# 138 extra 128x128 products of constants on TensorE in the two mixing stages of a diffusion trunk

## The chip, the cores and the metric

The program runs on one core of one Trainium2 chip. A core has TensorE (PE in the profile; its weight loads are PEld), VectorE (DVE), ScalarE (ACT), GpSimd (POOL) and SyncE (SP, which issues most transfers). The metric is the device time of one execution in microseconds, lower is better. The kernel before took 1597.66 us, the median of three runs (1592.06 to 1597.91).

## The reference, cut to what matters

Two layers; in each a half-step SwiGLU, the token mixing, and another half-step SwiGLU, for 128 context tokens and 256 latent tokens (384 columns in all). Only the mixing is touched:

```python
def token_mix(h, lp, lam_init, ctx, pos):
    a_q, a_k, a_v, b_q, b_k, b_v, b_g, b_r, c_q, c_k, c_v = jnp.split(h @ lp['w_in'], offs, axis=-1)
    # a: 6 query heads of 64 over 2 key heads; c: 4 heads, each with two score maps of 48
    # latent tokens: rope_2d on a_q, a_k, c_q, c_k; their keys are the latent and the cached context keys
    out_a = gqa_attention(a_q, keys_a, vals_a)            # softmax(q k / 8) v
    o_b, s_f, s_b = gla_bidir(b_q, b_k, b_v, log_a_f, log_a_b, s0_f, s0_b)   # gated linear attention, chunks of 64
    out_b = rms_norm(o_b, lp['g_gla']) * jax.nn.silu(b_r)
    # c: w = softmax(q1 k1) - lam * softmax(q2 k2);  out_c = rms_norm(w v)
    out_c = rms_norm(diff_attention(c_q, keys_c, vals_c, lam), lp['g_c_out']) * (1.0 - lam_init)
    return jnp.concatenate([out_a, out_b, out_c], axis=-1) @ lp['w_out']
```

## The kernel before

Activations lie transposed, 128 features by 384 tokens. Every big product is made of three passes (`mm3`, lines 307 to 310): the fp32 weights are split into a high and a low part (ScalarE line 303, VectorE line 304), and high by high, high by low and low by high are added in PSUM. So the four SwiGLU stages (FFN) and the projections of the mixing are long rows of dense 128-row passes, while the attention itself is plain fp32, in which one call of `PE.matmul` is two passes in the trace (an xcount of 2).

The mixing (`mixing`, lines 561 to 1085) is cut into named stages, and `ORDER[l]` lists them by layer: projections (`wq`, `wk`, `bv`, `wa`, `wv` in `proj_m`), norms and rotary embedding with a transpose behind it (`a_rope`, `c_rope`, lines 1002 and 1035), the levels of the gated attention (`L0` to `L6`, `scores`, line 901: 32-row products), the four heads of the differential attention (`c0` to `c3`, `c_head`), the pairs of grouped heads (`p0` to `p2`, `a_probs`), and the output product over `wo`. The code is written in that order, and a scheduler that simulates the engines lays the instructions out: an instruction of a later stage may be put ahead where its operands and buffers are there, and on each engine the laid-out order is then fixed.

A head of `c_head` does, for each of two blocks of 128 queries: two score products on 64 rows (line 789), on each a maximum (VectorE, line 694), an exponential with its sum (ScalarE, line 697), a reciprocal, scaling (lines 794 and 797) and three transposes (line 721, copied out by ScalarE, line 722); then the products with the values (lines 801 and 803, 128 rows) and a sum of squares by a product with ones (line 807). PSUM has eight banks: three of the tag `mm` and `both` by turns for big products and scores, three of `ax` and `ada` for the rest; a bank is taken anew when its last reader is done.

`ones` and `ident` are 128x128 constants in SBUF.

Of the kernel before, what the change touches and what calls it, by code (L numbers as in the profile page):

```python
# [17 lines left out]
P = 128  # L18
# [4 lines left out]
T = SEQ + LAT  # L23
# [58 lines left out]
def _build(ctx, tc, nc, I, O):  # L82
# [224 lines left out]
    def mm3(ps, lh, ll, rh, rl, start, stop):  # L307
        PE.matmul(ps, lhsT=lh, rhs=rh, start=start, stop=False)  # L308
        PE.matmul(ps, lhsT=lh, rhs=rl, start=False, stop=False)  # L309
        return PE.matmul(ps, lhsT=ll, rhs=rh, start=False, stop=stop)  # L310

    def newton(pool, ss, n, scale, parts, tag):

        m = pool.tile([P, n], F32, tag=tag + "m", name="nm")[:parts]
        V.tensor_scalar(out=m, in0=ss, scalar1=scale, scalar2=EPS, op0=ALU.mult, op1=ALU.add)
        s = pool.tile([P, n], I32, tag=tag + "s", name="ns")[:parts]
        V.tensor_scalar(out=s, in0=m.bitcast(I32), scalar1=1, scalar2=None, op0=ALU.logical_shift_right)
        y = pool.tile([P, n], F32, tag=tag + "y", bufs=2, name="ny")[:parts]
        V.tensor_scalar(out=y.bitcast(I32), in0=s, scalar1=-1.0, scalar2=float(0x5f3759df), op0=ALU.mult, op1=ALU.add)
        mh = pool.tile([P, n], F32, tag=tag + "h", name="nh")[:parts]  # L320
        V.tensor_scalar(out=mh, in0=m, scalar1=-0.5, scalar2=None, op0=ALU.mult)
        for _ in range(3):
            a = pool.tile([P, n], F32, tag=tag + "a", name="na")[:parts]
            V.tensor_tensor(out=a, in0=y, in1=y, op=ALU.mult)
            V.tensor_tensor(out=a, in0=a, in1=mh, op=ALU.mult)
            y2 = pool.tile([P, n], F32, tag=tag + "y", bufs=2, name="ny")[:parts]
            V.scalar_tensor_tensor(out=y2, in0=a, scalar=1.5, in1=y, op0=ALU.add, op1=ALU.mult)
            y = y2
        return y
# [231 lines left out]
    def mixing(l, us, acc, nxt):  # L561
        turn["own"] = {"mm": ("both",), "ax": ("ada",)}
        r_ = make_rstd(acc)
        with tc.tile_pool(name=f"mix{l}", bufs=1) as mp:
# [3 lines left out]
            def t512(n=512):  # L568
                return mt([P, 512], "t5", N512)[:, :n]


            kta = mt([P, T], "kta")
            ktc = mt([P, 4, 512], "ktc")
# [33 lines left out]
                    S.activation(out=dst[:, a:b], in_=t[:, a:b], func=func, bias=bc[:, c:c + 1], scale=scale)  # L607

            def proj_m(name, n, kper):
                ps = [mmps()[:, :n] for _ in range(3)]  # L610
                for k0 in range(0, KT, kper):
                    w = load_split(I[name][l, k0 // kper], kper * n)
                    for k in range(k0, k0 + kper):
# [123 lines left out]
            def a_probs(i):  # L737

                pts = [mt([P, 3, LAT], "pt", NPT), mt([P, 3, LAT], *(("e", 3) if i else ("pt", NPT)))]
                for t in range(2):  # L740
                    pp = [mmps()[:, :T] for _ in range(2)]
                    for g in range(2):
                        r = slice(64 * g, 64 * g + 64)
                        PE.matmul(pp[g], lhsT=qta[r, i, (t + 1) * P:(t + 2) * P], rhs=kta[r, :], start=True, stop=True)
                    for g, (p, rs) in enumerate(map(smax, pp)):
                        S.activation(out=p, in_=p, func=AF.Copy, scale=rs)
                        to_pt(p.rearrange("p (a b) -> p a b", a=3), 3, pts[g][:, :, t * P:(t + 1) * P])
                return pts
# [34 lines left out]
            def c_head(h, oc, osq, pss):  # L783
                pt = mt([P, 3, LAT], "pt", NPT)
                for t in range(2):
                    pp = [(mmps if PMM[4] else axps)()[:, :T] for _ in range(2)]
                    for m in range(2):
                        r = slice(64 * m, 64 * m + 64)
                        PE.matmul(pp[m], lhsT=qtc[r, h, (t + 1) * P:(t + 2) * P], rhs=ktc[r, h, 0:T],  # L789
                                  start=True, stop=True)  # L790
                    (p0, r0), (p1, r1) = map(smax, pp)
                    V.tensor_tensor(out=r1, in0=r1, in1=nl, op=ALU.mult)
                    if NRM[1]:
# [99 lines left out]
            sc = [mt([P, 2, 3, P], f"sc{i}") for i in range(2)]  # L893

            def scores(q, k, h, cross):
                ps = (mmps if PMM[10] else axps)()[:, :192].rearrange("p (c t) -> p c t", c=3)
                r = slice(32 * h, 32 * h + 32)
                for c in range(3):
                    for f in range(2):
                        fq = 1 - f if cross else f  # L900
                        PE.matmul(ps[64 * f:64 * f + 64, c, :], lhsT=k[r, c * P + 64 * f:c * P + 64 * f + 64],  # L901
                                  rhs=q[r, c * P + 64 * fq:c * P + 64 * fq + 64], start=True, stop=True)
                return ps

            def gla_diag():
# [75 lines left out]
                    V.tensor_tensor(out=lo, in0=ot[:, i, :], in1=hi.bitcast(F32), op=ALU.subtract)  # L981
                    mob.append((P, hi, lo))

            sv = {}

            def a_proj():
                pa = proj_m("wa", 512, 2)
                sv["a"] = qk_norm(pa, ((0, 6, 64, gq[:, 0:64]), (384, 2, 64, gq[:, 64:128])), 8, 64)
# [1 line left out]
            def a_rope():  # L990
                xa, ra = sv["a"]
                for t in range(3):
# [4 lines left out]
                    else:  # L997
                        xr = xa[0].rearrange("p h d -> p (h d)")
                        nc.sync.dma_start(out=O["nak"][l], in_=xr[:, 384:512])
                    ps = (mmps if PMM[13] else axps)()  # L1000
                    for i in range(4):
                        PE.transpose(ps[:, i * P:(i + 1) * P], xr[:, i * P:(i + 1) * P], ident)
                    S.activation(out=qta[:, :, t * P:(t + 1) * P],
# [17 lines left out]
            def c_rope(w):  # L1021
                xc, rc = sv[w]
                for t in range(3):
# [6 lines left out]
                    else:  # L1030
                        V.tensor_tensor(out=xc[t], in0=xc[t], in1=rc[t], op=ALU.mult)
                        rope(pad[:, :, 0:48], xc[t], 8, 48, t - 1, K_CC, K_SC)
                    ps = (mmps if PMM[13] else axps)()
                    for h in range(4):
                        PE.transpose(ps[:, h * P:(h + 1) * P], pad[:, 2 * h:2 * h + 2, :].rearrange("p a b -> p (a b)"),
                                     ident)
# [34 lines left out]
            acc = new_acc()  # L1071
            us = []
            for m in range(KT):
                ps = mmps()[:, :T]
                for k0, k1 in ((0, 5), (5, 9)):
                    w = load_split(I["wo"][l, m][:, k0 * P:k1 * P], (k1 - k0) * P)
                    for k in range(k0, k1):
# [141 lines left out]
```

## Time and profile before

| | |
|---|---|
| profiled execution | 1599.75 us |
| its span (first to last instruction) | 1597.9 us |
| TensorE busy | 1563.3 us (98%) |
| VectorE, ScalarE, GpSimd busy | 1229.3 (77%), 738.8 (46%), 196.2 (12%) us |
| mean granted TensorE clock | 0.980 of full |
| chain that ended last | TensorE 90%, VectorE 6%, ScalarE 2% |

The page gives busy time, the span in 40 slices with the granted clock, the chain of waits and the costliest groups. TensorE's ends are modelled, so a busy TensorE need not stream at its peak. The clock has two levels, 2.4 GHz (1.00 in the profile) and 1.2 GHz (0.50). Slices 10 to 13 (to about 520 us) and 28 to 33 (from about 1110 to 1290 us) hold the two mixings.

### The profile page before, as it was taken

What the parts mean: (1) busy time and instruction counts of PE and PEld (TensorE: products, weight loads), DVE (VectorE), ACT (ScalarE), POOL (GpSimd) and SP (SyncE); (2) the same over time, 40 slices, a digit from 0 to 9 for tenths busy, and PEclk for the clock granted to TensorE, in tenths of its full rate; (3) what the DMA queues carried; (4) which work ended last, traced back from release to release, by engine and by line L of the source; (5) the groups of instructions that cost most, each with busy time, mean ns of one, the idle gap of its engine ahead of it and who ended that gap; (6) DMA issues with size and microseconds to landing.
All of it is one profiled execution on the core that took longest, in us unless ns stands there. A gap on an engine that the chain in (4) does not pass through costs nothing.

```text
span 1597.9 us, 25055 instructions
## 1 busy us (share of the span) xinstructions
PE 1563.3 (98%) x9370; PEld 1464.0 (92%) x9370; DVE 1229.3 (77%) x2294; ACT 738.8 (46%) x1444; POOL 196.2 (12%) x239
## 2 busy tenths in 40 slices
PE   7999999999999999999999999999999999999999
PEld 5999999997558999999999999999875699999999
DVE  4799999888766888898968889667787767666532
ACT  4544433365466544443344444335546754444321
POOL 1211130030000211111001111102000011111100
PEclk9999999999789999999999999999898999999999
DMA  9677778542104566666666666543321064443441
GB/s 330 231 229 229 226 225 261 165 122 83 45 1 140 168 197 202 201 192 207 204 213 197 210 197 195 174 144 96 113 77 39 1 230 144 143 137 130 120 143 57
DMA packets 83230, 256.38 MB, mean 160 GB/s; under 512 B 10978, under 2 KB 19746, under 8 KB 82722
## 3 DMA queue, kind: packets, MB, share of 16 engines
q1 hardware_dynamic: 83108, 254.78, 50.3%
q8 instruction: 74, 1.21, 0.3%
q14 instruction: 48, 0.39, 0.1%
HBM read 251.99 MB, written 2.75 MB: 159 GB/s over the span
## 4 chain that ended last, share of the span: by engine, by line
PE 90%; DVE 6%; ACT 2%; issue 1%; DMA 1%; POOL 1%; SPq 0%; DVEq 0%; ACTq 0%; POOLq 0%
PE mm L308 20%; PE mm L310 20%; PE mm L309 20%; PE both L308 7%; PE both L309 7%; PE both L310 7%; PE mm L789 1%; DVE wlo L304 1%; PE ax L803 1%; PE ax L901 1%; PE ax L721 1%; DVE junk L254 1%; PE ax L807 0%; DVE ht L397 0%; PE ax L758 0%
## 5 line engine op out<-in xcount | busy, mean ns | idle before, releaser
L303 ACT ACTIVATE whi<-wraw 128x1024 fp32r<-128x1024 f32 (+4 forms) x358 | 348.4, 975 | 461.2 <-PE mm L309 259.1
L304 DVE TENSOR_TENSOR wlo<-wraw,whi 128x1024 fp32r<-128x1024 f32 (+4 forms) x358 | 451.8, 1264 | 131.0 <-ACT whi L303 129.0
L310 PE MATMUL mm<-h,wlo 128*128 128x386 f32 x1096 | 373.3, 341 | 2.5 <-DVE wlo L304 2.5
L308 PE MATMUL mm<-h,whi 128*128 128x386 f32 x1096 | 372.8, 341 | 2.6 <-POOL h L367 1.4
L309 PE MATMUL mm<-h,whi 128*128 128x386 f32 x1096 | 372.5, 340 | 0.0
L254 DVE SCALAR_TENSOR_TENSOR junk<-araw,cb 128x1024 f32<-128x1024 f32 x256 | 312.3, 1220 | 0.8
L310 PEld LDWEIGHTS mm<-h,wlo 128*128 128x128 f32 x1096 | 208.0, 190 | 4.2 <-DVE wlo L304 3.5
L308 PEld LDWEIGHTS mm<-h,whi 128*128 128x128 f32 x1096 | 207.6, 190 | 4.6 <-ACT whi L303 1.7
L309 PEld LDWEIGHTS mm<-h,whi 128*128 128x128 f32 x1096 | 207.6, 189 | 1.6 <-issue 0.7
L477 POOL TENSOR_TENSOR alo<-s,ahi 128x384 fp32r<-128x384 f32 x88 | 115.5, 1314 | 641.5 <-ACT ahi L475 614.9
L309 PE MATMUL mm<-alo,whi 128*128 128x384 f32 x528 | 177.9, 337 | 0.0
L310 PE MATMUL mm<-ahi,wlo 128*128 128x384 f32 x528 | 177.9, 337 | 0.0
L308 PE MATMUL mm<-ahi,whi 128*128 128x384 f32 x528 | 177.9, 337 | 0.0
L308 PE MATMUL both<-h,whi 128*128 128x386 f32 x360 | 122.5, 340 | 0.0
L309 PE MATMUL both<-h,whi 128*128 128x386 f32 x360 | 122.1, 339 | 0.0
L310 PE MATMUL both<-h,wlo 128*128 128x386 f32 x360 | 122.0, 339 | 0.0
L475 ACT ACTIVATE ahi<-s 128x384 fp32r<-128x384 f32 x88 | 46.3, 526 | 129.4 <-DVE s L472 129.3
L309 PEld LDWEIGHTS mm<-alo,whi 128*128 128x128 f32 x528 | 99.2, 188 | 0.0
L310 PEld LDWEIGHTS mm<-ahi,wlo 128*128 128x128 f32 x528 | 99.2, 188 | 0.0
L308 PEld LDWEIGHTS mm<-ahi,whi 128*128 128x128 f32 x528 | 99.2, 188 | 0.0
L469 DVE TENSOR_TENSOR u<-mm,rstd 128x384 f32<-128x384 f32 x66 | 36.6, 554 | 60.8 <-PE mm L310 60.8
L467 ACT ACTIVATE s<-s,bc 128x128 f32<-128x128 f32 (+1 forms) x176 | 70.7, 449 | 8.0 <-ACT bc L418 0.7
(365 smaller groups left out, 2446.7 us busy)
## 6 DMA issues: line engine op xcount, KB each, us to landing
wraw<-in_wgu SPq DMA_DIRECT2D x170, 512.0 KB, 4.2
araw<-in_w_adat SPq DMA_DIRECT2D x128, 512.0 KB, 4.0
wraw<-in_wd SPq DMA_DIRECT2D x64, 512.0 KB, 4.2
wraw<-in_wd SPq DMA_DIRECT2D x32, 384.0 KB, 3.5
araw<-in_w SPq DMA_DIRECT2D x16, 512.0 KB, 5.6
wraw<-in_wo SPq DMA_DIRECT2D x16, 320.0 KB, 3.0
wraw<-in_wit SPq DMA_DIRECT2D x8, 512.0 KB, 3.4
wraw<-in_wa SPq DMA_DIRECT2D x8, 512.0 KB, 3.6
```

Of the source, the lines that this page charges most:

```text
L254: V.scalar_tensor_tensor(out=junk, in0=w, scalar=1.0, in1=self.cb[:, c, :], op0=ALU.mult, op1=ALU.mult, accum_out=self.acc[:, f, c:c + 1])
L303: S.activation(out=hi[:, :cols], in_=raw[:, :cols], func=AF.Copy)
L304: vi = V.tensor_tensor(out=lo[:, :cols], in0=raw[:, :cols], in1=hi[:, :cols].bitcast(F32), op=ALU.subtract)
L308: PE.matmul(ps, lhsT=lh, rhs=rh, start=start, stop=False)
L309: PE.matmul(ps, lhsT=lh, rhs=rl, start=False, stop=False)
L310: return PE.matmul(ps, lhsT=ll, rhs=rh, start=False, stop=stop)
L467: S.activation(out=s[:, a:b], in_=s[:, a:b], func=AF.Silu, bias=bg[:, c:c + 1])
L469: vi = V.tensor_tensor(out=u, in0=pu[:, :T], in1=r, op=ALU.mult)
L475: S.activation(out=hi, in_=s, func=AF.Copy)
L477: G.tensor_tensor(out=lo, in0=s, in1=hi.bitcast(F32), op=ALU.subtract)
L721: pi = PE.transpose(ps[:, i * P:(i + 1) * P], p[:, i, :], ident)
L789: PE.matmul(pp[m], lhsT=qtc[r, h, (t + 1) * P:(t + 2) * P], rhs=ktc[r, h, 0:T], start=True, stop=True)
```

## The change

A helper `warm(ps, n, c)` issues n products of `ones` with `ident` into 128 columns of a PSUM tile that nobody reads, from column c on (384 by default, behind the 384 columns that scores use). Sixty-nine are issued in each mixing: 4 into the first bank of the first `proj_m`; 1 after each two of four heads' scores in the gated attention, so 2 in each of its eight rounds; 8 before the first scores of head `c0`; 1 on each score tile of the heads (16) and of the grouped heads (12); 1 before each rotary transpose (9); 4 before the first output product. The score tiles are therefore taken whole and cut to 384 columns afterwards; else nothing is changed.

```diff
+    def warm(ps, n, c=384):
+        for _ in range(n):
+            PE.matmul(ps[:, c:c + P], lhsT=ones, rhs=ident, start=True, stop=True)
...
             def proj_m(name, n, kper):
-                ps = [mmps()[:, :n] for _ in range(3)]
+                ps = [mmps() for _ in range(3)]
+                if not sv.setdefault("pm", 0):
+                    warm(ps[0], 4, 0)
+                sv["pm"] += 1
+                ps = [p[:, :n] for p in ps]
...
             def a_probs(i):
...
+                    for p in pp:
+                        warm(p, 1)
...
             def c_head(h, oc, osq, pss):
                 pt = mt([P, 3, LAT], "pt", NPT)
                 for t in range(2):
-                    pp = [(mmps if PMM[4] else axps)()[:, :T] for _ in range(2)]
+                    pp = [(mmps if PMM[4] else axps)() for _ in range(2)]
+                    if h == t == 0:
+                        warm(pp[0], 8)
                     for m in range(2):
...
+                    for p in pp:
+                        warm(p, 1)
+                    pp = [p[:, :T] for p in pp]
                     (p0, r0), (p1, r1) = map(smax, pp)
...
             def scores(q, k, h, cross):
-                ps = (mmps if PMM[10] else axps)()[:, :192].rearrange("p (c t) -> p c t", c=3)
+                bk = (mmps if PMM[10] else axps)()
+                ps = bk[:, :192].rearrange("p (c t) -> p c t", c=3)
...
+                if h % 2:
+                    warm(bk, 1)
...
                     ps = (mmps if PMM[13] else axps)()
+                    warm(ps, 1)          # in a_rope and in c_rope, before the transposes
...
             for m in range(KT):
-                ps = mmps()[:, :T]
+                ps = mmps()
+                if m == 0:
+                    warm(ps, 4)
+                ps = ps[:, :T]
```

The lines of the changed file are 5 to 25 higher; the products are its line 315. Three places of TensorE's order follow.

Where head `c0` begins in layer 0, before: the last level rounds (line 901), the scores of `c0` (line 789) and the first transposes (line 721).

```order
L901 MATMUL ax<-e 64x64 x6
L901 MATMUL ada<-e 64x64 x6
L901 MATMUL ax<-e 64x64 x12
L789 MATMUL mm<-ktc,qtc 128x384 x2
L789 MATMUL both<-ktc,qtc 128x384
L789 MATMUL mm<-ktc,qtc 128x384 x3
L789 MATMUL both<-ktc,qtc 128x384
L789 MATMUL mm<-ktc,qtc 128x384
L721 MATMUL ax<-cst,p 128x128 x3
```

The same place now (901 is 921, 789 is 805, 721 is 732).

```order
L921 MATMUL ax<-e 64x64 x12
L315 MATMUL ax<-cst 128x128
L315 MATMUL mm<-cst 128x128 x8
L805 MATMUL mm<-ktc,qtc 128x384 x2
L315 MATMUL mm<-cst 128x128 x2
L805 MATMUL both<-ktc,qtc 128x384
L805 MATMUL mm<-ktc,qtc 128x384
L315 MATMUL both<-cst 128x128
L315 MATMUL mm<-cst 128x128
L805 MATMUL mm<-ktc,qtc 128x384 x2
L315 MATMUL mm<-cst 128x128 x2
```

Eight products stand before the first scores, and a pair behind each pair of scores, ahead of the first transposes.

A little later, before: `c0`'s transposes, three scores of head `c1` put ahead, and `c0`'s products with the values (801, 803).

```order
L801 MATMUL ax<-ptx,cv 96x128
L789 MATMUL mm<-ktc,qtc 128x384 x2
L721 MATMUL ada<-cst,p 128x128 x3
L789 MATMUL both<-ktc,qtc 128x384
L803 MATMUL ax<-pt,cv 96x256 x3
L901 MATMUL ada<-e 64x64 x6
L789 MATMUL mm<-ktc,qtc 128x384
L807 MATMUL ax<-pt,cst 96x384
L901 MATMUL ax<-e 64x64 x12
```

The same place now (801 is 820, 803 is 822, 807 is 826).

```order
L805 MATMUL mm<-ktc,qtc 128x384
L315 MATMUL mm<-cst 128x128
L805 MATMUL both<-ktc,qtc 128x384
L822 MATMUL ax<-pt,cv 96x256 x3
L921 MATMUL ada<-e 64x64 x6
L315 MATMUL ada<-cst 128x128
L805 MATMUL mm<-ktc,qtc 128x384
L826 MATMUL ax<-pt,cst 96x384
L921 MATMUL ax<-e 64x64 x18
L315 MATMUL ax<-cst 128x128
L732 MATMUL ax<-cst,p 128x128 x3
```

The third score tile of `c1` (`both`) is still ahead, but the product in its bank is not: it stands further down, behind all that is shown here.

At the rotary transposes of `wk` in layer 0, before (1035 are the transposes, 309 and 310 passes of the projection `wa`).

```order
L901 MATMUL ax<-e 64x64 x18
L901 MATMUL ada<-e 64x64 x6
L1035 MATMUL ax<-cst,t_4125 128x128 x4
L309 MATMUL mm<-wlo,h 128x512
L310 MATMUL mm<-whi,h 128x512
L1035 MATMUL ax<-cst,t_4135 128x128 x4
```

The same place now (1035 is 1057).

```order
L921 MATMUL ada<-e 64x64 x6
L315 MATMUL ada<-cst 128x128
L315 MATMUL ax<-cst 128x128
L1057 MATMUL ax<-cst,t_4136 128x128 x4
L315 MATMUL ax<-cst 128x128
L1057 MATMUL ax<-cst,t_4147 128x128 x4
L315 MATMUL ax<-cst 128x128
```

A product stands right before each group of four transposes, and the passes that stood between two groups now stand behind both.

## Rows read from the trace of the kernel before

**Rows 1.** Page, parts 0 and 2: span, and granted clock in 40 slices

```profile
span 1597.9 us, 25055 instructions
...
PEclk9999999999789999999999999999898999999999
```

**Rows 2.** Windows at the low clock: start:end, length, busy us (instructions), clock, DMA

```profile
387.40:390.80 3.40, 3.40 (x16) 2.89 (x15) 3.05 (x7) 1.84 (x11) 0.00 (x0) 0.50 0.44 150
421.50:448.80 27.30, 26.83 (x112) 13.60 (x110) 15.07 (x46) 14.27 (x37) 0.00 (x0) 0.50 0.00 1
479.50:482.90 3.40, 3.40 (x11) 2.35 (x10) 2.81 (x6) 3.22 (x10) 0.00 (x0) 0.50 0.02 5
1118.00:1121.20 3.20, 3.20 (x15) 3.20 (x15) 2.71 (x5) 0.29 (x1) 0.00 (x0) 0.50 0.60 156
1128.10:1134.80 6.70, 6.70 (x30) 6.14 (x31) 4.59 (x14) 3.90 (x11) 0.00 (x0) 0.50 0.02 7
1179.30:1182.60 3.30, 3.30 (x12) 2.19 (x12) 2.12 (x6) 0.60 (x1) 0.00 (x0) 0.50 0.32 84
1213.40:1227.00 13.60, 13.60 (x42) 6.66 (x42) 7.26 (x23) 8.01 (x21) 0.00 (x0) 0.50 0.00 0
1271.50:1274.80 3.30, 3.30 (x13) 3.30 (x13) 1.44 (x4) 2.71 (x8) 0.00 (x0) 0.50 0.00 0
sum 64.20, PE 63.73 PEld 40.32 DVE 39.04 ACT 34.83 POOL 0.00; mean PE 7.97 PEld 5.04 DVE 4.88 ACT 4.35 POOL 0.00
```

**Rows 3.** Windows: a projection, two before a fall, one cold, warm heads

```profile
392.00:414.00 22.00, 22.00 (x98) 17.80 (x98) 20.01 (x45) 8.91 (x12) 2.37 (x2) 1.00 0.21 58
418.10:421.40 3.30, 0.84 (x5) 0.49 (x4) 3.25 (x11) 1.48 (x5) 0.00 (x0) 1.00 0.45 141
430.00:448.00 18.00, 18.00 (x92) 9.68 (x91) 8.66 (x26) 8.15 (x21) 0.00 (x0) 0.50 0.00 0
...
1124.70:1128.00 3.30, 3.30 (x45) 2.07 (x44) 1.54 (x3) 3.27 (x7) 0.00 (x0) 1.00 0.56 187
1228.00:1264.00 36.00, 35.03 (x320) 21.41 (x318) 28.18 (x100) 28.57 (x80) 2.01 (x4) 1.00 0.01 2
```

**Rows 4.** Timeline of TensorE before the fall at 1128: start, us, engine, line, shapes

```profile
1125.32 0.91 PE L634 MATMUL ax<-p 32*128 32x384 f32 x2
...
1126.80 1.26 PE L901 MATMUL ax<-qk 32*64 32x64 f32 x36
```

**Rows 5.** Timeline of TensorE, line 803 alone: one row each head

```profile
431.18 2.87 PE L803 MATMUL ax<-pt,cv 128*96 128x256 f32 x6
...
444.37 2.87 PE L803 MATMUL ax<-pt,cv 128*96 128x256 f32 x6
...
452.35 1.53 PE L803 MATMUL ax<-pt,cv 128*96 128x256 f32 x6
...
1231.42 1.54 PE L803 MATMUL ax<-pt,cv 128*96 128x256 f32 x6
...
1237.80 1.53 PE L803 MATMUL ax<-pt,cv 128*96 128x256 f32 x6 [0.47 <-ACT pt L722]
```

**Rows 6.** Chain of waits in order of time: one 128-column product, cold and warm

```profile
425.56 0.43 PE ax L801 x2
...
1230.44 0.22 PE ax L801 x2
```

**Rows 7.** Timeline of TensorE: its waits, in brackets, with what ended them

```profile
381.00 0.63 PE L1035 MATMUL ax<-cst,t 128*128 128x128 f32 x4 [0.82 <-DVE t L688]
...
420.65 1.96 PE L789 MATMUL mm<-ktc,qtc 64*128 64x384 f32 x4 [2.46 <-ACT p L697]
...
477.46 0.91 PE L744 MATMUL both<-kta,qta 64*128 64x384 f32 x2 [1.62 <-ACT e L965]
...
1117.05 0.40 PE L309 MATMUL mm<-wlo,h 128*128 128x288 f32 x1 [1.88 <-DVE wlo L304]
...
1211.38 2.03 PE L789 MATMUL mm<-ktc,qtc 64*128 64x384 f32 x6 [1.15 <-ACT p L697]
```

More of the change, by code (lines that the diff above doesn't have):

```diff
@@ L569, in t512 @@
                 return mt([P, 512], "t5", N512)[:, :n]
+            sv = {}
             kta = mt([P, T], "kta")
@@ L740, in a_probs @@
                 for t in range(2):
-                    pp = [mmps()[:, :T] for _ in range(2)]
+                    pp = [mmps() for _ in range(2)]
                     for g in range(2):
                         r = slice(64 * g, 64 * g + 64)
-                        PE.matmul(pp[g], lhsT=qta[r, i, (t + 1) * P:(t + 2) * P], rhs=kta[r, :], start=True, stop=True)
-                    for g, (p, rs) in enumerate(map(smax, pp)):
+                        PE.matmul(pp[g][:, :T], lhsT=qta[r, i, (t + 1) * P:(t + 2) * P], rhs=kta[r, :], start=True,
+                                  stop=True)
+                    for p in pp:
+                        warm(p, 1)
+                    for g, (p, rs) in enumerate(smax(p[:, :T]) for p in pp):
                         S.activation(out=p, in_=p, func=AF.Copy, scale=rs)
@@ L785, in c_head @@
                 for t in range(2):
-                    pp = [(mmps if PMM[4] else axps)()[:, :T] for _ in range(2)]
+                    pp = [(mmps if PMM[4] else axps)() for _ in range(2)]
+                    if h == t == 0:
+                        warm(pp[0], 8)
                     for m in range(2):
                         r = slice(64 * m, 64 * m + 64)
-                        PE.matmul(pp[m], lhsT=qtc[r, h, (t + 1) * P:(t + 2) * P], rhs=ktc[r, h, 0:T],
+                        PE.matmul(pp[m][:, :T], lhsT=qtc[r, h, (t + 1) * P:(t + 2) * P], rhs=ktc[r, h, 0:T],
                                   start=True, stop=True)
+                    for p in pp:
+                        warm(p, 1)
+                    pp = [p[:, :T] for p in pp]
                     (p0, r0), (p1, r1) = map(smax, pp)
@@ L982, in gla_out @@
                     mob.append((P, hi, lo))
-            sv = {}
             def a_proj():
@@ L1033, in c_rope @@
                     ps = (mmps if PMM[13] else axps)()
+                    warm(ps, 1)
                     for h in range(4):
```

## The prediction, made before the changed kernel was run

> **What bounds the kernel now.** I read the page first. TensorE is busy for nearly all of the span of 1597.9 us, and its granted clock is full but for a few slices, all in the two mixings [rows 1]. So the question is what those slices cost, and the windows view, cut until a window held one level only, answers it: TensorE ran at 1.2 GHz in eight stretches, 64.2 us together, and in them it was busy for 63.7 us [rows 2]. Two are long: 27.3 us over the heads c0 and c1 in layer 0, and 13.6 us over c0 in layer 1. The other six hold 23.3 us (3.4 + 3.4 + 3.2 + 6.7 + 3.3 + 3.3).
>
> What did the engine do before each fall? Two kinds of stretch are seen. Before 421.5 it stood nearly idle: 0.84 us busy of 3.30, since scores waited 2.46 us for a score bank that ScalarE's exponential held [rows 3, 7]. The same wait, 1.15 us, stands before 1213.4, and others of 1.62 and 1.88 us stand before 479.5 and 1118 [rows 7]. But before 1128.1 it was busy for 3.30 of 3.30 us [rows 3]; only its products were 32 rows high (32\*128, 32\*64) [rows 4]. And in the 18 us from 430 it never paused (18.00 busy) and stayed at 0.50 throughout [rows 3]. So what the engine does counts, not only whether it does something. The added products use all 128 rows and columns.
>
> By the Trainium skill (TensorE: Matmul & The Clock Gate, section "Why this matters for your kernels") a TensorE kept busy without pauses gets the full clock. The windows of 18.00 of 18.00 us at 0.50 say otherwise. By that rule alone only the products that fill a pause could help, and the 46 in and beside the heads would be pure cost; I go by the windows.
>
> **The change part by part.** It removes nothing and adds 138 products, 69 a mixing. Each is one fp32 call with 128 moving columns, so two passes. The nearest row is line 801, one such call: 0.22 us on the chain at full clock, 0.43 us at half [rows 6]. All 138 at full clock are 30.4 us; that is the upper bound of the cost while the clock is full, and nothing, if all of them lie in waits, is the lower one.
>
> *What the clock gives back.* In the heads, the products with the values (line 803) mark the period. Cold, c0 to c1 took 444.37 - 431.18 = 13.2 us; warm, c1 to c2 in layer 1 took 1237.80 - 1231.42 = 6.4 us; layer 0's c1 to c2, which began cold and ended warm, took 452.35 - 444.37 = 8.0 us [rows 5]. I take 8.0, since each head now has more to do and the other engines have their own work: in the 27.3 us VectorE is busy for 15.07 and ScalarE for 14.27 [rows 2], so no less than 15.1 us of it can remain. The ratio 8.0 / 13.2 makes 27.3 us into 16.5 (10.8 saved, at most 12.2), and 13.6 us into 8.2 (5.4 saved, at most 6.8). Together 16.2 us, between 0 (the clock stays) and 19.0.
>
> The six short stretches lie in projections or at the output product, with TensorE busy from end to end [rows 2], so half of each would come back: 11.7 us if all six went. I count three as gone (387.4, 479.5, 1271.5: products of the levels, of the rotary transposes and of the grouped heads fall right before them): 10.1 us of low clock, 5.0 us saved. Before 1128.1 and 1179.3 only a few are added, so I count half of them: 10.0 us, 2.5 saved. The one at 1118 follows a wait in the middle of a projection for split weights (1.88 us, VectorE [rows 7]) where no product is placed: nothing. Sum 7.5 us, and the clock gives back 23.7 us in all.
>
> *What the products cost*, at 0.22 us each:
> - 16 before the two c0: 3.5 us. TensorE waits 2.46 and 1.15 us right behind these scores [rows 7], 3.6 us together, so they cost nothing; without those waits 3.5. The scores come later by 8 x 0.22 = 1.8 us, while VectorE, busy for 3.25 of 3.30 us there [rows 3], still has level work and a weight split ahead of the first maximum.
> - 22 in dense projections: 18 beside the levels up to L2 (layer 0) and L3 (layer 1), and 4 at wq. TensorE is busy for 22.00 of 22.00 us in such a stretch [rows 3]. All on the path: 4.8 us.
> - 46 in and beside the heads, 10.1 us. In warm heads TensorE is busy for 35.03 of 36 us by its modelled ends, VectorE for 28.18 and ScalarE for 28.57 [rows 3]; the chain goes to and fro between the three. I take half: 5.1 us, between 0 and 10.1.
> - 24 on the grouped heads' scores and 8 before the output product: the same mixture, half of 7.0, so 3.5 us.
> - 18 before rotary transposes, 4.0 us. They need only a bank, not the rotated tile, so they can run while the transposes wait (0.82 us at one [rows 7]); where dense passes would have filled the place they are on the path. Half: 2.0 us.
> - 4 at bv in layer 1, where norms and weight splits set the pace (the wait of 1.88 us [rows 7]): nothing.
>
> That is 138 products and 15.4 us.
>
> *What they make wait.* In the changed program each of the 56 maxima (line 694 before) waits for the product behind its scores, though it reads other columns: a reader of a bank stands behind every write to that bank. On the chain that is up to 2 x 0.22 us for each of 28 pairs, 12.3 us if every pair were on it and none beside TensorE's own delay; VectorE's later maxima and the exponential are queued behind it. Half of that is already in the halves above (the chain passes either through the product or through the wait for it), so I add nothing and keep 6 us for the range. The third score tile of c1 is moved worse: its product stands behind c0's value products and level rounds, so that maximum comes some microseconds later. It is c1's, not due until c0's transposes are done, so I price it at nothing; if due, it costs up to one warm value product and sum of squares, some 2.5 us.
>
> The Trainium skill (PSUM: Partial Sum Buffer, section "PSUM bank collisions raise a hardware error") asks for semaphores by bank rather than by address; no trace of before shows what such a wait costs here. By that rule the wait can't be had away with other columns, and the 6 us stay in the range.
>
> The DMAs issued are the same in number and size; some weight loads change places with each other, and the waits shown end on VectorE and ScalarE [rows 7]: nothing. The four FFN stages are at full clock and get no products.
>
> **The sum.** -23.7 + 15.4 = -8.3 us against the profiled execution of 1599.75 us, whose span is 1597.9: 1591.4. The median of the runs shown is 1597.66, so I forecast 1589 us.
>
> **The rivals.**
> - *All the clock comes back and the products mostly lie in waits.* For it: the waits before the falls are where the products were put, and warm heads go at 6.4 us. Then 16.2 + 11.7 = 27.9 us come back at a cost of 7.7: 1577 us. Against it: TensorE has few idle microseconds to hide anything.
> - *Break-even.* Heads recover, the short stretches only move: each product shifts the work, and a fall elsewhere takes the place of one prevented. 16.2 back, 15.4 spent: 1597 us. For it: the six short ones have six different causes.
> - *The products do not lift the clock* (slower). The stretch from c0 stays at 0.50 because between two products there is as much 64- and 32-row work as before; then each of the 18 products there takes 0.43 us on a chain that is TensorE's alone, 7.7 us, and the rest cost 4.8 + 3.1 (28 beside heads, half) + 3.5 + 2.0 = 13.4: 21 us more, 1619 us. It decides if the clock is 0.50 for more than 20 us behind the first product before c0. For it: 18 us of unbroken work at 0.50 [rows 3]; against it: the wait before 421.5, which began that stretch, is filled with products, and behind 448.8 the same work went on at full clock.
> - *The products are dropped*, since nobody reads them: they stand in the order of the changed program on TensorE, so I give this nothing.
>
> **How the numbers follow.** The sum as worked out has 0.43, full recovery 0.27, break-even 0.13, products that don't lift the clock 0.17. A difference under 0.5% (8 us) can't be told from none here. The forecast lies at that bound: of its 0.43 I put 0.26 beyond it and 0.17 within (with it break-even's 0.13). So faster 0.53, same 0.30, slower 0.17. The range: at the low end full recovery with a little more hidden, 1574; at the high end break-even plus the 6 us of later maxima and 2.5 of the moved tile, rounded up to 1607; the forecast's own range is 1580 to 1597.
>
> **What would show it.** Right: the mean granted clock above 0.99; at c0 of both layers no wait of TensorE over 1 us and no fall behind it; the period of line 803's successor in layer 0 from c0 to c1 near 8 us; the products at 0.22 us a call. Wrong: the clock at 0.50 behind c0 (the third rival); falls at new places (break-even); or heads at full clock with a period over 10 us, which would mean that VectorE and ScalarE, or the maxima that wait for products, set the pace and the half is too small a share.

## The result: 0.7% slower, at a clock that rose as forecast

The changed kernel takes 1604.92 us (median of 9, 1604.11 to 1609.68) beside 1592.06 us for the kernel before on the same chip (9, 1588.15 to 1600.92). The ratio is 1.0069, 95% interval 1.0046 to 1.0091: slower. The forecast was 1589 us; the time lies inside the range given (1574 to 1607), but on the wrong side of no change. Executions over 1.5% slower than the fastest of their kernel are left out of all figures; there were two, of 1616.70 us (two heads and c0, below) and 2341.44 us (change, maxima first).

The page of the changed kernel's profiled execution (1605.07 us): span, TensorE, and the granted clock in 40 slices.

```profile
span 1603.3 us, 25613 instructions
...
PE 1578.5 (98%) x9646; PEld 1485.9 (93%) x9646; DVE 1233.4 (77%) x2294; ACT 737.7 (46%) x1444; POOL 195.4 (12%) x239
...
PEclk8999999999999999999999999999999999999999
```

The low slices of [rows 1] are gone; the first slice is low now: the clock was 0.50 for 6.8 us from 12.3 and for 3.4 us from 36.2, in a stage before the mixings that the change does not touch. Windows of the same trace: start:end, length, busy us (instructions) of TensorE, weight loads, VectorE, ScalarE, GpSimd, then clock, DMA share, GB/s. The two mixings, then c0 and c1 of layer 0, heads of layer 1, and the one low stretch left in a mixing.

```profile
316.40:539.90 223.50, 220.61 (x1575) 181.88 (x1574) 170.01 (x428) 132.64 (x301) 27.97 (x40) 0.98 0.29 90
1099.90:1323.40 223.50, 218.74 (x1574) 178.50 (x1573) 170.85 (x428) 133.08 (x301) 26.43 (x40) 1.00 0.29 92
422.80:450.00 27.20, 26.96 (x203) 16.37 (x203) 20.20 (x66) 16.16 (x42) 0.00 (x0) 1.00 0.04 10
...
479.50:486.30 6.80, 6.80 (x18) 3.67 (x16) 3.77 (x10) 4.76 (x14) 0.00 (x0) 0.53 0.01 2
1214.00:1255.00 41.00, 40.60 (x316) 25.74 (x312) 26.49 (x88) 25.71 (x70) 1.11 (x3) 1.00 0.00 1
```

So both long falls of the clock in [rows 2], 27.3 and 13.6 us, are gone, and five of the six short ones; that at 479.5 is now 6.8 us long. The mixings as a whole, before (from 314.6 to 535.8 and from 1095.8 to 1318.0 us):

```profile
314.60:535.80 221.20, 214.22 (x1437) 170.09 (x1436) 167.56 (x428) 133.50 (x301) 28.27 (x40) 0.92 0.29 91
1095.80:1318.00 222.20, 210.73 (x1436) 169.26 (x1435) 169.27 (x428) 133.33 (x301) 26.70 (x40) 0.93 0.30 92
```

These four rows hold the answer. Before, TensorE was busy for 424.95 us in both mixings and idle for 18.45. The clock took 0.08 x 221.2 + 0.07 x 222.2 = 33 us of the busy time (32.4 by windows of 0.5 us), so at whole clock it is 392.5. Now it is busy for 439.35 and idle for 7.65; the clock takes 3.4 (half of the 6.8), so 436 at whole clock. **The 138 products added 43 us of TensorE time, 0.31 us each, not the 0.22 that the prediction took, and the idle time shrank by 11 us.**

The products with the values (line 822, before 803), one row each head, answer to [rows 5].

```profile
434.17 1.54 PE L822 MATMUL ax<-pt,cv 128*96 128x256 f32 x6
...
441.21 1.54 PE L822 MATMUL ax<-pt,cv 128*96 128x256 f32 x6
...
448.69 1.53 PE L822 MATMUL ax<-pt,cv 128*96 128x256 f32 x6
...
1222.83 1.53 PE L822 MATMUL ax<-pt,cv 128*96 128x256 f32 x6
1231.95 1.54 PE L822 MATMUL ax<-pt,cv 128*96 128x256 f32 x6
1240.33 1.54 PE L822 MATMUL ax<-pt,cv 128*96 128x256 f32 x6
```

In layer 0 the period from c0 to c1 fell from 13.2 to 7.0 us. In layer 1, where c1 was already warm, c1 to c2 rose from 6.4 to 8.4 us. The heads went warm (to the whole clock), and where they had been warm already they became dearer.

The chain of waits in order of time (start, us, what; x2 is the two passes of one product) answers to [rows 6].

```profile
435.70 0.49 PE ada L921 x12
436.19 0.42 PE ada L315 x2
436.61 0.84 PE mm L805 x2
...
438.94 0.56 PE ax L921 x12
439.50 0.42 PE ax L315 x2
...
440.58 0.22 PE ax L820 x2
440.80 0.22 PE both L315 x2
441.02 0.22 PE mm L315 x2
```

A product behind work on 128 rows (line 820) takes 0.22 us. Behind a level's round on 32 rows (line 921) it takes 0.42. Read over both mixings, 26 products stand on the chain directly behind line 921, each at 0.42 to 0.43; those directly behind scores on 64 rows (lines 805 and 755) nearly all take 0.42 too, and a second product behind the first 0.22. The row that set the price in the prediction, line 801, stands behind transposes on 128 rows.

The same holds off the chain. Taken product by product from the timeline of TensorE over both mixings, each from the end of what ran before it, without idle time and with half-clock time halved, the 138 take 42.3 us: 56 stand directly behind work on 32 or 64 rows and take 0.42 each, and nearly all of the other 82 take 0.22. All other work of TensorE takes the same as before, within 1 us of 393. So the 43 us are the products' own time.

The Trainium skill (TensorEngine Tiling (Array Packing), "Tiling Modes", "Key Properties") says that a change of tiling mode drains the engine. The trace agrees in so far as the step from 32 or 64 rows to 128 costs some 0.2 us. It does not show that a drain is the cause; about half of the 0.2 us can be seen as a weight load that does not run ahead. Behind line 921 a product (PE) and its load (PEld) start together, and behind line 820 the load starts 0.11 us earlier:

```profile
436.12 0.49 PE L315 MATMUL ada<-cst 128*128 128x128 f32 x2
436.12 0.30 PEld L315 LDWEIGHTS ada<-cst 128*128 128x128 f32 x2
440.63 0.39 PE L315 MATMUL both<-cst 128*128 128x128 f32 x2
440.52 0.30 PEld L315 LDWEIGHTS both<-cst 128*128 128x128 f32 x2
```

TensorE's one wait of over 0.3 us from c0 to the grouped heads of layer 0 (us in total, times, longest) answers to [rows 7]:

```profile
PE both L755 <- ACT e L987: 1.0, 1, 1.0
```

and, of all products, who waited for them (us in total, times):

```profile
  DVE mx L705: 5.2, 7
  DVE sd L959: 4.8, 9
  POOL t L1046: 1.2, 1
```

### The profile page after: what moved, and what is told of

Same layout as the page of the kernel before. It is cut to its first block, busy times and chain, and to the rows that moved or that the text cites. A ratio compares the mean times of both kernels' runs of the same rounds, so it can differ in the third digit from the quotient of the medians.

```text
span 1603.3 us, 25613 instructions
## 1 busy us (share of the span) xinstructions
PE 1578.5 (98%) x9646; PEld 1485.9 (93%) x9646; DVE 1233.4 (77%) x2294; ACT 737.7 (46%) x1444; POOL 195.4 (12%) x239
## 4 chain that ended last, share of the span: by engine, by line
PE 90%; DVE 6%; ACT 1%; issue 1%; DMA 1%; POOL 0%; SPq 0%; DVEq 0%; POOLq 0%; ACTq 0%
PE mm L308 20%; PE mm L309 20%; PE mm L310 20%; PE both L308 7%; PE both L310 7%; PE both L309 7%; DVE wlo L304 1%; PE ax L921 1%; PE mm L315 1%; PE mm L805 1%; PE ax L732 1%; PE ax L822 1%; DVE junk L254 1%; PE ax L315 1%; PE mm L755 1%
```

## The experiments

Each was timed in five rounds beside the kernel before. One scale serves them all. In 150 executions of the program before, each with its own granted clock (0.978 to 0.990), the time is a straight line: **1573.2 us at whole clock and 1.375 us more for each 0.001 of clock lost**, with a typical distance of 0.9 us and a largest of 3.2. So a run's cost at equal clock is its time less that line at its own clock. Above 0.990 the line is continued; two variants reached 1.000 once each, and there their distance to it (13.4 and 19.2 us) is that of their means (13.6 and 19.0).

| run | products | median us | ratio to before, 95% | mean clock | us over the line | each |
|---|---|---|---|---|---|---|
| change | 138 | 1604.92 | 1.0069 (1.0046-1.0091) | 0.9966 | 27.7 | 0.20 |
| before again | 0 | 1597.46 | 0.9992 (0.9972-1.0012) | 0.984 | 0 | |
| products ahead | 138 | 1612.14 | 1.0087 (1.0066-1.0109) | 0.9927 | 27.7 | 0.20 |
| none on heads | 82 | 1604.37 | 1.0063 (1.0033-1.0092) | 0.9887 | 16.6 | 0.20 |
| only ahead of c0 | 16 | 1601.30 | 1.0039 (1.0017-1.0060) | 0.9831 | 4.6 | 0.29 |
| one pass | 138 | 1619.76 | 1.0150 (1.0120-1.0180) | 0.9805 | 19.8 | 0.14 |
| twice | 276 | 1633.80 | 1.0236 (1.0209-1.0264) | 0.9958 | 55.1 | 0.20 |
| heads only | 56 | 1607.06 | 1.0052 (1.0022-1.0082) | 0.9872 | 13.6 | 0.24 |
| in the FFN | 128 | 1620.97 | 1.0158 (1.0127-1.0188) | 0.9850 | 27.2 | 0.21 |
| heads and c0 | 72 | 1599.09 | 1.0020 (0.9994-1.0046) | 0.9923 | 13.7 | 0.19 |
| c_head and c0 | 48 | 1598.48 | 1.0032 (1.0009-1.0054) | 0.9896 | 11.1 | 0.23 |
| two heads and c0 | 32 | 1592.48 | 1.0019 (0.9992-1.0045) | 0.9883 | 5.7 | 0.18 |
| no levels | 106 | 1597.32 | 1.0023 (1.0003-1.0044) | 0.9963 | 19.0 | 0.18 |
| only c0, maxima first | 16 | 1592.17 | 0.9979 (0.9952-1.0007) | 0.9895 | 3.3 | 0.21 |
| change, maxima first | 138 | 1604.59 | 1.0072 (1.0048-1.0096) | 0.9971 | 28.3 | 0.21 |
| two heads, maxima first | 32 | 1588.47 | 0.9964 (0.9937-0.9990) | 0.9909 | 3.3 | 0.10 |
| heads, maxima first | 72 | 1594.31 | 1.0002 (0.9977-1.0026) | 0.9947 | 13.3 | 0.19 |
| before, maxima first | 0 | 1598.41 | 1.0001 (0.9976-1.0025) | 0.9835 | 0.3 | |
| two heads, maxima first, again | 32 | 1587.82 | 0.9960 (0.9937-0.9983) | 0.9916 | 3.9 | 0.12 |

**The kernel before, once more,** with no edit.

> The kernel before, unchanged, to see how its time hangs on the granted clock. Theory A (where the falls of the clock lie differs from execution to execution, and the profiled one had many): the executions spread from about 1588 to 1600 us, the clock from about 0.99 to 0.98, lower clock with longer time, and the profile of a fast one lacks one of the two long stretches at 1.2 GHz. Theory B (the spread has another cause): the same clock, 0.980 within 0.001, in fast and slow executions.

Its 12 times run from 1589.67 at 0.988 to 1600.92 at 0.978. The time hangs on the clock.

**The products ahead of the scores of their bank,** in `c_head` and in `a_probs`:

```diff
                     pp = [(mmps if PMM[4] else axps)() for _ in range(2)]
+                    for p in pp:
+                        warm(p, 1)
...
-                    for p in pp:
-                        warm(p, 1)
```

> As the changed kernel, but the products on the score tiles of c_head and a_probs are written ahead of the scores of their bank instead of behind them; number and size are the same. Theory A (late maxima: the scheduler puts a product behind lower stages' work, and the maximum of that bank waits for it): 4 to 8 us faster than the changed kernel's 1605, so 1597 to 1601, with the period of the heads in layer 1 back under 8 us from 8.4 to 9.1. Theory B (the price of the products on TensorE alone): the same 1603 to 1607, since TensorE does the same work.

No maximum waits for a product any more (behind the change they waited 5.2 us), and the cost at equal clock is the same 27.7 us. But another wait takes the place of that one: the products now stand behind the exponential that frees their bank, and TensorE is idle before them (us in total, times; 0.4 us in the change).

```profile
  ACT p L708: 12.7, 23
```

TensorE's own time on the products is much as in the change, 43.1 us counted in the same way. So theory B fits, and the order of score and product does not matter to the sum; what the late maxima cost by themselves this run does not show.

**No products on the score tiles of the heads** (both loops of `warm(p, 1)` taken out):

> As the changed kernel without the 56 products on the score tiles of c_head and a_probs (82 are left). Theory A (late maxima): 8 to 14 us faster than 1605, near 1593, if the clock stays over 0.99. Theory B (price on TensorE alone, 0.42 us for a product that stands alone, half of them on the path): 56 x 0.42 / 2 = 12 us, near 1593 too, and e2 tells the two apart. Rival C (the clock needs them): clock back to 0.985, time 1595 to 1605.

82 products cost 16.6 us, so the 56 cost 11.1 us on top of them, and the clock scatters from 0.977 to 0.994. Part of the heads' clock needs the 56 (rival C); the price fits A and B alike.

**Only the products ahead of c0:** all other calls of `warm` taken out.

> Only the 8 products before the first scores of head c0 in each mixing, 16 in all. Theory A (they fill the wait behind which the clock fell, and cost nothing else): the long stretches at 1.2 GHz go, 1580 to 1586 us. Theory B (they push the scores of c0 and the maxima behind them): about as before, 1588 to 1596, with the first scores some 2 us or more later. Rival C (other products kept the clock up): clock near 0.98, 1595 to 1600.

Alone they cost 4.6 us where the prediction had nothing, and bring the clock nothing (0.983, before 0.984). TensorE's longest waits from c0 on, before and here:

```profile
PE mm L789 <- ACT p L697: 2.5, 1, 2.5
```

```profile
PE mm L803 <- ACT p L708: 2.6, 2, 1.9
```

The wait that was to hide them is still there. Why, the timelines of VectorE show. Before, c0's maxima (line 694) come right behind the last level's copy, and the next gate (line 923) behind three of them:

```profile
419.07 0.36 DVE L937 COPY_PREDICATED sd<-msk,ax 128x192 f32<-128x192 uint8 x1
419.34 1.01 DVE L694 TENSOR_REDUCE mx<-mm 128x1 f32<-128x384 f32 x2
420.27 0.54 DVE L694 TENSOR_REDUCE mx<-both 128x1 f32<-128x384 f32 x1
...
420.81 0.34 DVE L923 TENSOR_TENSOR e<-c 128x192 f32<-128x192 f32 x1
```

With the 16 products all four gate subtractions are laid ahead of the first maximum, since the scores are due later:

```profile
420.74 0.36 DVE L953 COPY_PREDICATED sd<-msk,ax 128x192 f32<-128x192 uint8 x1
421.00 0.35 DVE L939 TENSOR_TENSOR e<-c 128x192 f32<-128x192 f32 x1
...
421.81 0.35 DVE L942 TENSOR_TENSOR e<-c 128x192 f32<-128x192 f32 x1
422.08 0.55 DVE L705 TENSOR_REDUCE mx<-mm 128x1 f32<-128x384 f32 x1
```

**One pass in place of two:** the operands of all 138 rounded to f32r, in which each product is one record in the trace, not two.

```diff
+    cr = const.tile([P, P], F32R, name="cr")
...
-            PE.matmul(ps[:, c:c + P], lhsT=ones, rhs=ident, start=True, stop=True)
+            PE.matmul(ps[:, c:c + P], lhsT=cr, rhs=cr, start=True, stop=True)
```

> All 138 products stay where the change put them, but each runs in one pass on operands rounded to f32r instead of two passes in f32 (one more VectorE copy of the identity at the start of the first mixing). A, the price is TensorE time on the path, two passes of 0.11 us: half of it goes, 138 x 0.11 = 15 us, and with the clock still whole the time is about 1605 - 15 = 1590 us. B, the price is in each product's weight load or in the waits it causes, not in its passes: the time stays at 1602 to 1606. C, the products lift the clock only by the time they fill: half as long, they leave some stretches low again (granted clock 0.985 to 0.990 in place of 0.997), and 1590 becomes 1594 to 1600.

Half the passes save 0.06 us of 0.20 by the line; in the trace the products take 22.8 us of TensorE in place of 42.3, 0.12 behind a product and 0.24 to 0.26 behind narrow work. So the second pass is about half of TensorE's time but less than a third of the price on the path. The clock came out below that of the kernel before (0.9805), which none of the three theories had: it falls again, in layer 1 (windows of its trace):

```profile
1213.50:1227.10 13.60, 13.55 (x35) 7.70 (x36) 6.61 (x23) 7.98 (x23) 0.00 (x0) 0.50 0.00 0
1247.50:1281.60 34.10, 34.10 (x178) 21.17 (x172) 14.66 (x42) 15.54 (x44) 2.02 (x4) 0.50 0.00 1
```

The second is 34.10 us of unbroken work at half clock. The rule weighed in the prediction (the Trainium skill, TensorE: Matmul & The Clock Gate, "Why this matters for your kernels") that a busy TensorE gets the full clock does not hold here either.

**Each product twice:**

```diff
-        for _ in range(n):
+        for _ in range(2 * n):
```

> Each of the 138 products is written twice, 276 in all, in the same places; the clock has nothing more to win. A, every product costs its 0.22 us on the path, hidden nowhere: 138 x 0.22 = 30 us more than the change, about 1635. B, half of it lies in TensorE's waits, as the prediction summed: 15 more, about 1620. C, the price is the change from work on 64 rows to work on 128 and back, so that a second product behind the first is nearly free: 1605 to 1610.

The second 138 cost 27.4 us, as the first 138 did. They stand behind a product, so none needs a change of height, and they find nothing to hide in: the windows of its mixings show 478.10 - 469.57 = 8.5 us of idle time, after 7.65 in the change. Less 8.5 us for the clock TensorE is busy for 461, so the second ones took 25 us of it, 0.18 each beside the 0.31 of the first.

```profile
316.40:555.90 239.50, 236.41 (x1712) 198.03 (x1712) 172.35 (x428) 133.48 (x301) 28.00 (x40) 0.98 0.26 84
1115.90:1354.50 238.60, 233.16 (x1712) 195.44 (x1711) 173.18 (x428) 134.04 (x301) 26.44 (x40) 0.99 0.27 86
```

**Heads only:** the 56 products on score tiles, all others taken out.

> Only the 56 products on the score tiles of both kinds of heads are left; the 82 before c0, beside the gated levels and rotary transposes and at the joints are gone. A, the price is linear and on the path: the program before at whole clock, about 1574 by its line of time on clock, plus 56 x 0.22 = 12 gives 1586 at whole clock, and 4.5 us more for each 0.01/1.6 us... that is for each 10 us of low clock: at 0.990 about 1592. B, the products on the heads are dearer than the others, since the maxima and levels wait behind them (1604 of the change less 1593 without them at whole clock is 11, the same as 56 x 0.2): then 1600 or more. C, they hold the clock through the heads by themselves: granted 0.990 or more; otherwise it stays at 0.982 to 0.986 as before.

13.6 us at equal clock, near the 12 of theory A, and clocks from 0.984 to 1.000 with a mean of 0.987, so C does not hold. At 1.000 the one execution took 1586.6. In the profiled one the long fall at c0 is there as before:

```profile
423.50:450.70 27.20, 27.20 (x106) 15.09 (x104) 12.74 (x38) 11.72 (x33) 0.00 (x0) 0.50 0.00 1
```

**In the FFN:** none in the mixings, 128 alone between dense passes in the four down stages.

```diff
+                        if k in (0, 6, 12, 18):
+                            warm(axps(), 1)
```

> The kernel before with 128 of the same products put into the four down stages of the FFN instead of the mixings, each alone between passes on 128 rows, on a tile that nobody reads, where TensorE runs without a gap at whole clock; nothing in the mixings. It measures a product's price where nothing can hide it and no clock can be won. A, 0.22 us each as in the chain of before: 28 us, from 1595 to about 1623 at the same granted clock of 0.982 to 0.986. B, a lone product costs 0.33 to 0.42 as after's chain shows beside scores: 42 to 54, about 1640 to 1650. C, the weight load and one of the passes go under the neighbour: 14 or less, about 1609.

27.2 us, 0.21 each (0.22 each in the trace), among work on 128 rows and with no wait near. That is the price of line 801, so the prediction's price is right for such a place.

**Fewer products:** the heads' 56 and c0's 16; then without those on the grouped heads; then only c_head's first two heads; and the change without those beside the levels.

```diff
                 if h % 2:
-                    warm(bk, 1)
+                    pass
```

> 72 products are left: the 56 on the score tiles of both kinds of heads and the eight ahead of c0 in each mixing. Linear price: the line of the program before (1573 us at whole clock, 1.38 us more for each 0.001 of granted clock lost) plus 72 x 0.20 = 14 gives 1588 at whole clock. A, these two places are all that the heads' clock needs: granted 0.995 or more, 1590 to 1595, a little under before. B, the levels and the joints are needed as well: 0.984 to 0.990 as with the 56 alone, 1601 to 1610. C, the price depends on the place: at equal clock off the line plus 14 by more than 3.

> 48 products are left: 32 on the score tiles of c_head and the eight ahead of c0 in each mixing; the grouped heads have none. Linear price: the line of before plus 48 x 0.20 = 10, so 1583 at whole clock. A, the fall at c0 is held off by products on c_head alone: granted 0.994 or more, 1586 to 1592. B, clock as before, 0.982 to 0.986: 1602 to 1608.

> 32 products are left: on the score tiles of c_head's first two heads and the eight ahead of c0. Linear price: the line of before plus 32 x 0.20 = 6, so 1580 at whole clock. A, a few products at the place of the fall suffice: granted 0.992, 1590. B, clock as before, 0.982 to 0.986: 1599 to 1604. If the price is linear at every clock, the time lies within 3 us of the line plus 6.

> The change without the 32 products beside the gated levels, 106 left. Linear price: the line of before plus 106 x 0.20 = 21, so 1594 at whole clock. A, the level products are not needed for the clock: granted 0.996, 1600. B, they are: 0.985 to 0.990, 1608 to 1615. If the maxima and gates that wait behind the level products are what costs, it falls below the line plus 21 by several us.

None beats the kernel before. The level products are not needed for the clock (0.9963 without them) and are the dearest group: 27.7 - 19.0 = 8.7 us for 32, most of which stand behind work on 32 rows. Each of the sets lies within another, so the differences give a price by place.

| place | products | predicted us | measured us |
|---|---|---|---|
| ahead of c0 | 16 | 0 | 4.6 |
| score tiles of c_head | 32 | 3.5 | 11.1 - 4.6 = 6.5 |
| score tiles of the grouped heads | 24 | 2.6 | 13.7 - 11.1 = 2.6 |
| wq, bv, rotary transposes, output | 34 | 3.8 | 19.0 - 13.7 = 5.3 |
| beside the levels | 32 | 5.5 | 27.7 - 19.0 = 8.7 |
| sum | 138 | 15.4 | 27.7 |

These prices hold for this order of adding only. The 16 ahead of c0 cost 4.6 us alone, but on top of the heads' 56 they cost nothing that can be measured (13.7 beside 13.6 us) and raise the mean clock from 0.987 to 0.992. So the term that the prediction put at nothing is near nothing where the heads have products too. The heads' 56 cost 13.6 us alone, 9.1 on top of c0's 16 and 11.1 on top of the other 82. Why they overlap is not shown.

**Maxima first:** VectorE's order at c0 held as before, so that the gates of the next level stand behind c0's first two maxima; first with the 16 alone, then with the change, with 32 and with 72 products.

```diff
+                    if h == t == 0:
+                        sv["hold"] = sv["mx"].ins
...
+                hold = sv.pop("hold", None) if li == (5, 6)[l] else None
+                with tc.issue_after(hold) if hold is not None else ExitStack():
                     V.tensor_tensor(out=ev[:, 0, :, :, 1, :], in0=cut(c0, 1)[:, :, :, 1, :], in1=mid(c0), op=ALU.subtract)
```

> The 16 products ahead of c0 alone, as in the run with 16, but VectorE's order is held: the four gate subtractions of the next level stand behind c0's first two maxima, as in the kernel before, not ahead of them. A, the 16 cost 4.6 us over the line of before because VectorE does gate work (4 x 0.27 us) ahead of the maxima, so that the wait for the score bank stays (2.6 us) and the products are not in it: held, the wait shrinks under 1.5 us and the cost falls to 1 to 2 us over the line, the time at 1594 to 1598 at 0.984 to 0.986. B, the price is TensorE's own time ahead of the scores: 3.5 to 4.6 over the line as before, whatever VectorE does.

The waits at c0, in the same window as the 2.6 us above, shrink to 1.3 us, the longest to 0.7:

```profile
PE mm L803 <- ACT p L708: 1.3, 2, 0.7
```

and the cost shrinks from 4.6 to 3.3 us. The idle time of the mixings falls from 18.5 (before, and with the 16 alone) to 15.8. So VectorE's order was part of it, some 1.3 us; the remaining 3.3 are above the 1 to 2 that theory A gave, and what holds them is not settled. Its clock came out higher as well, 0.9895 (0.983 with the 16 alone). The two profiled executions show where: with the 16 alone the clock is 0.50 behind c0 in both layers, and with the order held it is whole there. A fall of 23.9 us lies later, from 450.7.

```profile
425.00:438.50 13.50, 12.67 (x34) 6.53 (x36) 7.60 (x25) 7.78 (x23) 0.00 (x0) 0.50 0.01 1
1210.00:1223.60 13.60, 13.25 (x41) 6.60 (x42) 5.33 (x18) 7.61 (x21) 0.00 (x0) 0.50 0.00 1
```

```profile
421.00:450.00 29.00, 27.38 (x268) 15.87 (x270) 26.13 (x87) 22.91 (x61) 0.00 (x0) 1.00 0.04 10
1205.00:1235.00 30.00, 28.84 (x211) 16.79 (x210) 24.72 (x81) 22.44 (x63) 0.00 (x0) 1.00 0.09 28
```

> The change with its 138 products and VectorE's order at c0 held in the same way. A: some 3 us less than the change, 1601 to 1602 at 0.997. B: the same as the change, 1604 to 1605. C, held gates make the next level late and TensorE waits for it: 1607 or more.

The order changes nothing here: with products on the score tiles as well, the wait at c0 was already down to 0.2 us in the change. B holds there.

> 32 products (c0's eight and the score tiles of the first two heads) and VectorE's order at c0 held. It took 5.9 us over the line with granted clock 0.987. A: 3 over the line, so 1589 to 1593 if the clock is the same, a little under before. B: 6 over, 1594 to 1596.

> 72 products (c0's eight and all score tiles) and VectorE's order at c0 held. It took 13.8 us over the line at 0.992, 1599. A: 11 over, 1595 to 1596. B: 14 over, 1598 to 1600.

The version with 32 products is faster than the kernel before: 1588.47 us, ratio 0.9964 (0.9937 to 0.9990).

> The kernel before without any product, with VectorE's order at c0 held in the same way. It tells whether the gain of the version with 32 products comes from the hold or from the products. A, the products lift the clock and the hold only makes them cheaper: the time stays on the line of before at 0.984, 1593 to 1596. B, the hold itself is the gain: 3 us under the line or more, about 1588 to 1591.

> The version with 32 products and VectorE's order held, once more beside the kernel before, to see whether its gain holds: it took 1588.5 (ratio 0.9964, interval 0.9937 to 0.9990). If the gain is real, 1586 to 1591 with granted clock 0.989 to 0.992; if it was the draw of clocks, 1594 to 1597 at 0.985.

The order alone does nothing (1.0001). The version with 32 gains again: 0.9960 (0.9937 to 0.9983). It costs 3 to 4 us over the line and lifts the mean clock from 0.984 to 0.991, which is worth 10. Without the held order its clock was 0.988 and it gained nothing. That the order bears on the clock is seen with the 16 alone, where the falls behind c0 went; why they went is not shown, since the shorter wait came with other changes of order.

## Why the prediction was wrong, point by point

**Held: the clock.** The steps "the clock gives back 23.7 us" and "mean granted clock above 0.99" came true. From the profiled execution's 1599.75 us to the line at the change's mean clock, 1573.2 + 3.4 x 1.375 = 1577.9, it is 21.9 us. No wait over 1 us is left at c0, no fall behind it, and in the mixings no new fall took the place of an old one, so neither break-even nor the slower rival happened. The period from c0 to c1 is 7.0 us, near the 8.0 that the sum took.

**Partly luck of the draw: the base of the sum.** The 23.7 us were counted from an execution at 0.980. The mean of the 150 executions is 0.984, and the nine beside the change (1592.06 us) lie by the line at 0.986. From there the change gives back only 17 and 14 us. Even at the forecast cost of 15.4 us it would have been no faster than those nine, about 1593 us.

**Failed: "Each is one fp32 call ... The nearest row is line 801, one such call: 0.22 us", and with it "All 138 at full clock are 30.4 us; that is the upper bound".** They took 43 us of TensorE, 0.31 each: 0.22 behind work on 128 rows, 0.42 behind work on 32 or 64. The price was 12.6 us too little, and the miss of the cost term is 27.7 - 15.4 = 12.3. The sign that the prediction named, "the products at 0.22 us a call", failed with it. The row was chosen by shape, not by what stands ahead of it. The trace of before held the other price: the three passes of line 721 take 0.33 us behind line 807 (96 rows) and 0.48 behind line 901 (32 rows), in these rows of its chain.

```profile
1228.64 1.21 PE ax L901 x34
1229.85 0.48 PE ax L721 x3
...
1234.62 0.33 PE ax L721 x3
```

**Nearly held: the amount hidden.** The prediction hid 30.4 - 15.4 = 15 us in waits. The idle time fell by 18.45 - 7.65 = 10.8. At whole clock the kernel before would have idled more: 0.001 of clock over 1600 us is 1.6 us of TensorE time and by the line 1.375 us of the run, so 14% of what the clock gives back goes into waits, an estimate of some 4 us of the 29. With that 15 us were hidden, and 43 - 15 = 28 fits the 27.7. But part of it was laid in the wrong places: c0's 16 were to lie wholly in a wait that stands *behind* their scores. Alone they do not, since VectorE filled the time ahead of its maxima with gates, and with the order held 3.3 us of cost were still left; only on top of the heads' products did they cost nothing that can be measured.

**Not shown apart: the late maxima and the moved tile.** The prediction put them at nothing in the sum and kept 6 us in the range. With the products ahead of the scores the price is the same, but there other waits stand in their place. The cost can be accounted for without them.

**The sum again.** From the nine beside the change: 1592.06 - 14.2 + 27.7 = 1605.6; measured 1604.92. This only shows that the terms agree, since the 27.7 us are read from the same executions. The traces are a check of their own: 42.3 us of products, 29 us back from the clock and 10.8 us less idle time make the two mixings 2.5 us longer; they are 447.0 - 443.4 = 3.6 us longer. That the time lies inside the range is luck: the high end was made of break-even and the late maxima, and neither is what is seen.

## What to carry to other kernels

Price an added instruction by a row that has the same neighbour ahead of it, not only the same shape; on TensorE a full-height product behind 32- or 64-row work cost twice what it cost behind its own kind here (0.42 and 0.22 us). Before counting half of an added cost as hidden, take the idle time of the stage from the windows (18 us here) as a measure of what can hide, and see whether the work delays what the wait hangs on. Count what a change of clock can give back from the mean of many executions, not from one that drew a low clock. Where a throttle scatters the time, fit time on granted clock over many executions first: a change of 4 us can then be read in a scatter of 13.

## What the runs showed of the hardware that was not expected

- The same program drew mean clocks from 0.978 to 0.990 and times from 1586.6 to 1601.9 us; 0.001 of clock is 1.375 us, so 1 us of TensorE time lost to the clock costs 0.86 us here.
- 34.10 us of unbroken TensorE work at half clock, in the run with one-pass products.
- A change from 32- or 64-row work to 128 rows costs about 0.2 us, the same behind 32 as behind 64 rows.
- A product in one pass costs 0.14 us on the path, one in two passes 0.20.
- With the same 16 products the clock behind c0 was 0.50 for 13.6 us in each layer, or whole, by the order of VectorE's gates and maxima (one execution each).
